# A decoder layer on one core: W_s's row sums, the past rows' sums and the sample's mixing done another way, and the tables of the spatial step loaded later

## The chip, the cores and the metric

The kernel runs on one core of one Trainium2 chip. A core has TensorE (PE in the profile; PEld is its weight load), VectorE (DVE), ScalarE (ACT), GpSimd (POOL) and SyncE (SP), which issues DMAs. Each engine works through its own instructions in order; semaphores make one wait for another. The metric is the device time of one execution in microseconds (us), and the median of several executions is given.

## The reference

One layer works on a prompt of 1024 rows and on 8 sample rows (one new row for each of 8 sequences), 1024 wide, all in float32. Cut to what the change touches:

```python
proj = einsum('bld,de->ble', rmsnorm(h, pre_g), w_in)
u, v, z_a, x_b, z_b, g_a, g_b = split(proj, SPLITS)
vn = layernorm(gelu(v), ln_g, ln_b)
# within chunks of 128 rows, 8 heads of 128 channels
s = einsum('hts,bcshd->bcthd', tril(w_s), vn) + b_s
y_a = gelu(u) * s * silu(z_a)
# trailing windows of 2, 4, 8, 16 rows; a sample's past rows come from state_pool (8, 15, 1024)
pooled = mean_over_window(x_b) - x_b
y_b = (blockdiag(pooled, w_pool) * pool_scale) * silu(z_b)
m = sigmoid(g_a) * (y_a @ w_pa) + sigmoid(g_b) * (y_b @ w_pb)
h = h + rmsnorm(m @ w_out, post_g)
h = h + rmsnorm(sigmoid(rmsnorm(h, ple_in_g) @ w_pg) * (p @ w_ple), ple_out_g)
```

Three small things in it matter here. A sample row is the first row of its chunk, so its mixing is s = w_s[h, 0, 0] * vn + b_s[h, 0]. For the prompt, the scale and the shift of the layer norm are taken out of the mixing: with n the normalised rows, sum over s of W[t, s] * (g * n[s] + b) is g * (W n)[t] + b * rowsum(W)[t], so the row sums of the lower triangle of W_s are wanted once, as an offset `off` = b * rowsum(W_s) + b_s. And a sample's window needs the sum of the last 1, 3, 7 or 15 past rows, by channel group.

## The kernel before

The layer is a stream of about a hundred large products on PE. A product of float32 matrices is computed from two parts of each factor (ACT copies the high part, DVE subtracts it: `split`), three matmuls for each tile. `strassen` (line 632) makes seven products of a projection's pair of 128-column blocks, each accumulated over four k-tiles in one of three PSUM regions (tag `acc`), which DVE (`u<-acc,u`, `v<-acc,u`) or ACT (`u<-acc`) must empty before the region is used again. In its order P1, P6, P2, P7, P4, P5, P3, the last, P3, adds into the region that P5 has just filled and DVE has just read.

The stages follow each other: the four pairs of the v projection (`vsteps`), of the gate g_a (`gasteps`), of u and z_a (`usteps`), of x_b and z_b with the pooling (`bsteps`), of g_b, then the merges and the two last projections. V's output is transposed by the DMA engines: ACT splits it into 16-bit planes `vw`, SP issues one DMA transpose for each of the eight blocks (`v_planes`, 871), ACT joins the planes into `big` (`v_join`, 880) and applies gelu (`v_turn`, 889). In the gate stage the layer norm and the mixing are fitted in (`ln_stats`, `ln_apply`, `spatial`, 984).

Which instruction stands where is decided by a planner (class `Planner`, line 51). Every operation is recorded by `take` (146) with an estimated busy time and, for a DMA, its amount and the time until it has landed; `order` (202) then runs through the estimates and puts each engine's instructions in the order in which they would start. The order is fixed at build time; on the chip only the semaphores decide when something runs. A DMA on SP also waits until the DMA issued eight before it has landed. The first part of the program (`begin`, 1601) is kept in its written order, the rest is free.

The parts that the change touches: `small_tables` (1094, called at 1680 in `begin`) makes on POOL the eight diagonal tables `diag` for the sample's mixing and four 0/1 tables `mask` for the past rows. `ln_loads` (936) loads W_s (`ws`) and the layer norm's vectors, put at the second step of the first v pair (1278). `spatial_weights` (948) clears the upper triangle on POOL, transposes the eight heads on PE into the PSUM banks `psw` and splits them into `wst` (1279). `spatial_offsets` (965) forms the row sums by four products with a tile of ones (`rowsum`) and from them `off`. `sample_spatial` (1001) multiplies the eight sample rows by `diag` (`smix`). `pool_state` (1091) loads the 120 past rows into row block 7 of `big`, and `state_sums` (1112) sums them by eight products with `mask` (`state`) into `past`, which `window` (1132) reads.

Of the kernel before, what the change touches and what calls it, by code (L numbers as in the profile page):

```python
# [15 lines left out]
P = 128  # L16
# [39 lines left out]
class Planner:  # L56
# [89 lines left out]
    def take(self, engine, method, args, kwargs):  # L146
        given = [*(("out" if i == 0 else "", a) for i, a in enumerate(args)), *kwargs.items()]
        writes = [a for k, a in given if k in ("out", "accum_out") and a is not None]
        reads = [a for k, a in given if k not in ("out", "accum_out") and hasattr(a, "tensor")]
        if kwargs.get("accum_op") is not None:  # L150
            reads += writes
        name = writes[0].tensor.name
        if engine == "tensor" and self.open is not None and self.open[0] == name:
            op = self.open[1]
        else:
            op = Op(engine, len(self.ops), self.clock, self.fixed)
            self.ops.append(op)
        self.open = (name, op) if engine == "tensor" else None
        op.calls.append((method, args, kwargs))
        op.spent.append(op.busy)  # L160
        if method[:9] == "dma_start":
            op.busy, op.moved = 1.0 if engine == "gpsimd" else 0.45, writes[0].size() * (2e-6 if writes[0].dtype == U16 else 4e-6)
            op.lands = 4.5 if kwargs.get("accum_op") is not None else 2.0
        else:
            took = self.duration(engine, method, writes[0], reads, kwargs)
            op.busy += took
            if engine == "tensor" and not self.fixed:
                self.clock += took
            if engine == "scalar":
# [134 lines left out]
def hybrid_step(  # L304
# [643 lines left out]
    def spatial_weights():  # L948

        ws = lnt["ws"]  # L950
        nc.gpsimd.affine_select(out=ws, in_=ws, pattern=[[0, NB], [-1, P]], compare_op=ALU.is_ge,
                                fill=0.0, base=0, channel_multiplier=1)
        lnt["wst"] = []
        for h4 in range(0, NB, 4):
            w = slot("wst", (P, 4, 2, P), F32R)
            ps = bank("psw")
            for i in range(4):
                nc.tensor.transpose(ps[:, i * P : (i + 1) * P], ws[:, h4 + i, :], ident)
            split(ps.rearrange("p (h t) -> p h t", t=P), w[:, :, 0], w[:, :, 1])
            lnt["wst"].append(w)  # L960
        ps = bank("lncol")
        nc.tensor.transpose(ps[:, : 2 * NB], lnt["vec"][: 2 * NB, :], ident[: 2 * NB, : 2 * NB])
        nc.vector.tensor_copy(lncol, ps[:, : 2 * NB].rearrange("p (i k) -> p i k", i=2))

    def spatial_offsets():

        ones = slot("ones", (P, P), F32R)
        nc.gpsimd.memset(f32(ones), 1.0)
        off = lnt["off"] = slot("off", (P, NB, P))
        for h4, w in zip(range(0, NB, 4), lnt["wst"]):  # L970
            ps = bank("rowsum")
            for c in range(2):
                nc.tensor.matmul(ps.rearrange("p (h t) -> p h t", t=P), ones, w[:, :, c], start=c == 0, stop=c == 1)
            for h in range(h4, h4 + 4):
                c = slice(h * P, (h + 1) * P)
                nc.vector.scalar_tensor_tensor(out=off[:, h], in0=ps[:, (h - h4) * P : (h - h4 + 1) * P],
                                               scalar=lncol[:, 1, h : h + 1], in1=lnt["bs"][:, c],
                                               op0=ALU.mult, op1=ALU.add)

    def v_split(t):  # L980
        lnv["cut", t] = lnv["cut", t], slot("vl", (P, D), F32R)
# [19 lines left out]
    def sample_spatial():  # L1001
        ps = bank("smix").rearrange("p (h t) -> p h t", h=NB)
        for h in range(NB):
            nc.tensor.matmul(ps[:, h, :NS], sv[:NS, h * P : (h + 1) * P], lnt["diag"][:NS, h, :],
                             start=True, stop=True)
        first = lnt["bs"].rearrange("p (h t) -> p h t", h=NB)[:, :, :1]
        add(smix_s, ps[:, :, :NS], first.to_broadcast([P, NB, NS]))


    kept = {}  # L1010
# [5 lines left out]
    wgcut = {what: dram.tile([HALF, D], F32, tag="wg" + what, name="wg" + what) for what in ('T4', 'B22')}  # L1016
    kept["h"] = dram.tile([T, D], F32, tag="h", name="h")
    kept["e"] = dram.tile([T, D], F32, tag="e", name="e")

# [69 lines left out]
    masks = {}  # L1089

    def pool_state():
        dma(big[: NS * POOL_BUF, 7, :D], state.rearrange("b r d -> (b r) d"))

    def small_tables():

        w00 = lnt["w00"]
        diag = lnt["diag"] = cpool.tile([P, NB, NS], F32, tag="diag", name="diag")
        for h in range(NB):
            nc.gpsimd.tensor_scalar(out=diag[:, h, :], in0=ident[:, :NS], scalar1=w00[:, h : h + 1],
                                    scalar2=None, op0=ALU.mult)  # L1100
        for g, w in enumerate(WINDOWS):
            m = masks[g] = small.tile([P, NS], F32, tag="mask", name=f"mask{g}", bufs=NPAIR)
            nc.gpsimd.memset(m, 1.0)
            nc.gpsimd.affine_select(out=m, in_=m, pattern=[[-POOL_BUF, NS]], compare_op=ALU.is_ge,
                                    fill=0.0, base=w - 1 - POOL_BUF, channel_multiplier=1)
            nc.gpsimd.affine_select(out=m, in_=m, pattern=[[POOL_BUF, NS]], compare_op=ALU.is_ge,
                                    fill=0.0, base=POOL_BUF - 1, channel_multiplier=-1)

    state_sb, tail = big[:, 7, :D], big[:, 6, :D]
    past = cpool.tile([P, NB, NS], F32, tag="past", name="past")  # L1110

    def state_sums():

        n = NS * POOL_BUF
        ps = bank("state").rearrange("p (b t) -> p b t", b=NB)
        for b in range(NB):
            nc.tensor.matmul(ps[:, b, :NS], state_sb[:n, b * P : (b + 1) * P], masks[b // 2][:n, :],
                             start=True, stop=True)
        nc.vector.tensor_copy(past, ps[:, :, :NS])

    class XB(User):
        def tails(self):
# [152 lines left out]
    at(vsteps[1][0], lambda: xop.cut("T4"))  # L1275


    at(c[1], ln_loads)
    at(vsteps[1][2], spatial_weights)
    for i, u in enumerate(vusers):  # L1280

        nxt = vsteps[1][1:] + vsteps[2] if i == 0 else (vsteps[i + 1] if i + 1 < NPAIR else gasteps[0])
# [318 lines left out]
    def begin():  # L1601
# [130 lines left out]
```

## Time and profile before

| | us |
|---|---|
| median of 3 runs | 1000.1 (1000.04 to 1001.04) |
| the profiled execution | 997.51 |
| its span, first to last instruction | 995.8 |
| ACT busy in the span | 526.0 |
| DVE busy in the span | 800.5 |
| idle time of ACT before joining planes, ended by a DMA transpose | 8.4 |

The profile is of one execution, and all its times are from the first instruction of the span. A row of the timeline has start, length, engine, line, operation, tiles written<-read, shapes and a count; in brackets the idle time before it and what ended it. Line 297 is that of the helper that plays the recorded operations, so groups are told apart by their tiles.

### The profile page before, as it was taken

The numbers are of one execution on the slowest core, as the hardware profiler recorded it, in microseconds if no ns is written. First come the engines' busy times: TensorE is split into PE (matmuls) and PEld (weight loads), VectorE is DVE, ScalarE is ACT, GpSimd is POOL, SyncE is SP. The second block draws the span as 40 slices with busy tenths as digits, with TensorE's granted clock in tenths as the row PEclk, the third lists the DMA queues.
The fourth block names the chain that finished last, engine by engine and source line by source line (L and its number), as shares of the span: only waits on it lengthen the run. The fifth ranks groups of instructions, "written<-read, shape, count | busy, mean of one in ns | idle before, by whom it ended". The sixth has DMA issues, their size and how long they took to land. (4 is left out here: it accounts for less than half of the span.)

```text
span 995.8 us, 16069 instructions
## 1 busy us (share of the span) xinstructions
PE 981.3 (99%) x6136; PEld 881.0 (88%) x6136; DVE 800.5 (80%) x1241; ACT 526.0 (53%) x925; POOL 72.7 (7%) x162
## 2 busy tenths in 40 slices
PE   8999999999999999999999999999999999999996
PEld 6889989999999899999999999999999988888885
DVE  5975468777778888888897987697799798779796
ACT  7767888756434434243433343562353365677653
POOL 2200000000000000001000100000000002312111
PEclk9999999999999999999999999999999999999999
DMA  9334462232365355546635166874663553389646
GB/s 342 128 124 85 110 169 106 86 107 64 135 230 186 104 184 185 197 134 227 240 120 166 40 238 232 287 287 149 215 254 110 172 206 68 84 275 364 166 108 191
DMA packets 103970, 171.14 MB, mean 172 GB/s; under 512 B 24254, under 2 KB 64238, under 8 KB 103885
## 3 DMA queue, kind: packets, MB, share of 16 engines
q1 hardware_dynamic: 101525, 162.21, 47.9%
q0 software_dynamic: 2048, 7.37, 4.3%
q8 instruction: 48, 0.79, 0.3%
q10 hardware_dynamic: 320, 0.54, 0.2%
q14 instruction: 29, 0.24, 0.1%
HBM read 114.59 MB, written 51.77 MB: 167 GB/s over the span
## 5 line engine op out<-in xcount | busy, mean ns | idle before, releaser
L297 DVE TENSOR_TENSOR u<-acc,u 128x520 f32<-128x520 f32 (+1 forms) x90 | 62.6, 696 | 38.8 <-PE acc L297 36.8
L297 POOL TENSOR_TENSOR rstd<-ms,mhalf 128x1 f32<-128x1 f32 (+1 forms) x45 | 36.5, 812 | 213.6 <-DVE ms L297 213.5
L297 POOL MEMSET u<- 128x8 f32 x35 | 3.5, 105 | 558.1 <-PE acc L297 310.9
L297 ACT ACTIVATE u<-acc 128x512 f32<-128x512 f32 x39 | 23.2, 595 | 26.9 <-PE acc L297 26.4
L297 ACT ACTIVATE paw<-pas 128x512 fp32r<-128x512 f32 x16 | 10.1, 629 | 31.2 <-DVE pas L297 25.9
L297 ACT ACTIVATE pbw<-pbs 128x512 fp32r<-128x512 f32 x16 | 10.0, 630 | 28.2 <-DVE pbs L297 24.9
L297 DVE TENSOR_TENSOR big<-big 128x1024 f32<-128x1024 f32 (+4 forms) x20 | 23.6, 1217 | 0.0
L297 ACT ACTIVATE big<-v 128x1024 uint16<-128x1024 uint16 x16 | 18.5, 1173 | 8.4 <-DMA v<-vw 8.4
L297 ACT ACT_TABLE_LOAD x15 | 19.2, 1283 | 6.5 <-PE acc L297 5.5
L297 ACT ACTIVATE big<-pht,gvec 128x128 f32<-128x128 f32 x64 | 18.0, 381 | 8.1 <-PE pht L297 8.1
L297 ACT ACTIVATE big<-mix 128x256 f32<-128x256 f32 x32 | 12.2, 384 | 16.9 <-PE mix L297 16.2
L297 PE MATMUL accm<-qh,wpoolw 128*128 128x260 f32 (+1 forms) x96 | 20.9, 320 | 0.0
L297 DVE TENSOR_TENSOR acc<-acc,u 128x512 f32<-128x512 f32 (+1 forms) x16 | 11.2, 699 | 8.8 <-PE acc L297 8.8
L297 DVE TENSOR_TENSOR big<-mix,big 128x256 f32<-128x256 f32 x32 | 13.2, 422 | 5.9 <-ACT big L297 5.0
L297 ACT ACTIVATE zbw<-zbs 128x512 fp32r<-128x512 f32 x16 | 10.1, 632 | 14.6 <-DVE zbs L297 7.2
L297 ACT ACTIVATE zaw<-zas 128x512 fp32r<-128x512 f32 x16 | 10.0, 630 | 14.5 <-DVE zas L297 9.0
L297 ACT ACTIVATE gbw<-gbs 128x512 fp32r<-128x512 f32 x16 | 10.0, 626 | 13.9 <-DVE gbs L297 12.0
L297 PEld LDWEIGHTS accm<-qh,wpoolw 128*128 128x128 f32 x96 | 15.5, 188 | 1.9
L297 ACT ACTIVATE zbw<-zbraw 128x512 fp32r<-128x512 f32 x12 | 7.5, 627 | 17.8 <-DMA zbraw<-in_w_in_dram 16.3
L297 ACT ACTIVATE uw<-us 128x512 fp32r<-128x512 f32 x16 | 10.0, 627 | 12.3 <-DVE us L297 9.8
L297 ACT ACTIVATE junk<-ge 128x512 bf16<-128x512 f32 (+2 forms) x19 | 11.6, 609 | 8.9 <-DVE ge L297 8.3
L297 ACT ACTIVATE gb<-gb 128x1032 f32<-128x1032 f32 (+1 forms) x8 | 6.8, 854 | 17.6 <-DVE gb L297 17.6
(689 smaller groups left out, 3632.2 us busy)
## 6 DMA issues: line engine op xcount, KB each, us to landing
ga<-ga SPq DMA_DIRECT2D x16, 516.0 KB
gb<-gb SPq DMA_DIRECT2D x16, 516.0 KB
ya<-za SPq DMA_DIRECT2D x8, 516.0 KB
yb<-zb SPq DMA_DIRECT2D x8, 516.0 KB
x<-in_x_prompt_dram SPq DMA_DIRECT2D x8, 512.0 KB
vraw<-in_w_in_dram SPq DMA_DIRECT2D x8, 512.0 KB
e<-e SPq DMA_DIRECT2D x8, 512.0 KB
garaw<-in_w_in_dram SPq DMA_DIRECT2D x8, 512.0 KB
```

The source lines that it names most:

```text
L297: getattr(getattr(self.nc, e), method)(*args, **kwargs)
```

## The change

- The planner charges a DMA transpose 3.0 us of its engine (0.45 before), next to no amount, and 1.5 us to land.
- `ln_loads` moves to the fourth step of the third v pair, `spatial_weights` and `ln_rows` to the first step of the gate.
- Row sums of W_s: DVE reduces `ws` along s (128 x 8 sums), SP writes them to DRAM turned (8 x 128) and reads them back to all partitions into `off`; DVE multiplies and adds in place. The tile of ones and the four products go.
- Sample's mixing: eight transposes of the sample rows on PE, then DVE multiplies by w_s[h, 0, 0] and adds b_s[h, 0]. The tables `diag` go.
- Past rows: POOL clears row block 7 of `big`; ten DMAs place the rows that each window needs, for channel block k in partitions 8k to 8k+7 (eight latest rows in partitions 64 and up, earlier ones below); DVE reduces over the eight rows held by a partition; one product with `twice` (two identity blocks side by side, added) sums the two halves and transposes. The tables `mask` go, and `small_tables` with them.

```diff
@@ take
             op.lands = 4.5 if kwargs.get("accum_op") is not None else 2.0
+            if method == "dma_start_transpose":
+                op.busy, op.moved, op.lands = 3.0, 0.01, 1.5
@@ spatial_weights
+        sums = cpool.tile([P, NB], F32, tag="rowsums", name="rowsums")
+        nc.vector.tensor_reduce(out=sums, in_=ws, op=ALU.add, axis=mybir.AxisListType.X)
+        dma(kept["rowsum"].rearrange("h t -> t h"), sums)
@@ spatial_offsets
-        ones = slot("ones", (P, P), F32R)
-        nc.gpsimd.memset(f32(ones), 1.0)
         off = lnt["off"] = slot("off", (P, NB, P))
-        for h4, w in zip(range(0, NB, 4), lnt["wst"]):
-            ps = bank("rowsum")
-            for c in range(2):
-                nc.tensor.matmul(ps.rearrange("p (h t) -> p h t", t=P), ones, w[:, :, c], start=c == 0, stop=c == 1)
...
+        dma(off, kept["rowsum"].partition_broadcast(P))
+        for h in range(NB):
+            nc.vector.scalar_tensor_tensor(out=off[:, h], in0=off[:, h], scalar=lncol[:, 1, h : h + 1],
+                                           in1=lnt["bs"][:, h * P : (h + 1) * P], op0=ALU.mult, op1=ALU.add)
@@ sample_spatial
-            nc.tensor.matmul(ps[:, h, :NS], sv[:NS, h * P : (h + 1) * P], lnt["diag"][:NS, h, :],
-                             start=True, stop=True)
+            nc.tensor.transpose(ps[:, h, :NS], sv[:NS, h * P : (h + 1) * P], ident[:NS, :NS])
         first = lnt["bs"].rearrange("p (h t) -> p h t", h=NB)[:, :, :1]
-        add(smix_s, ps[:, :, :NS], first.to_broadcast([P, NB, NS]))
+        mul(smix_s, ps[:, :, :NS], lnt["w00"].unsqueeze(2).to_broadcast([P, NB, NS]))
+        add(smix_s, smix_s, first.to_broadcast([P, NB, NS]))
@@ pool_state
-        dma(big[: NS * POOL_BUF, 7, :D], state.rearrange("b r d -> (b r) d"))
+        rows_of = big[:, 7, :D].rearrange("p (r c) -> p r c", c=P)
+        nc.gpsimd.memset(rows_of, 0.0)
+        nc.vector.tensor_tensor(out=twice, in0=ident[:, : P // 2], in1=ident[:, P // 2 :], op=ALU.add)
+        for k in range(NB):
+            w = WINDOWS[k // 2] - 1
+            for j in range(2):
+                n = min(w, NB) if j else w - NB
+                if n > 0:
+                    first = POOL_BUF - n if j else POOL_BUF - w
+                    dma(rows_of[(j * NB + k) * NS : (j * NB + k + 1) * NS, NB - n :],
+                        state[:, first : first + n, k * P : (k + 1) * P])
@@ state_sums
-        n = NS * POOL_BUF
-        ps = bank("state").rearrange("p (b t) -> p b t", b=NB)
-        for b in range(NB):
-            nc.tensor.matmul(ps[:, b, :NS], state_sb[:n, b * P : (b + 1) * P], masks[b // 2][:n, :],
-                             start=True, stop=True)
-        nc.vector.tensor_copy(past, ps[:, :, :NS])
+        got = big[:, 4, :P]
+        nc.vector.tensor_reduce(out=got, in_=state_sb.rearrange("p (r c) -> p c r", c=P),
+                                op=ALU.add, axis=mybir.AxisListType.X)
+        ps = bank("state")
+        nc.tensor.matmul(ps[:, : P // 2], got, twice, start=True, stop=True)
+        nc.vector.tensor_copy(past, ps[:, : P // 2].rearrange("p (b t) -> p b t", b=NB))
@@ where the steps are put
-    at(c[1], ln_loads)
-    at(vsteps[1][2], spatial_weights)
+    at(vsteps[2][3], ln_loads)
+    at(gasteps[0][0], spatial_weights)
-    at(vsteps[3][0], ln_rows)
+    at(gasteps[0][0], ln_rows)
@@ begin
-        small_tables()
```

The changed numbers of the planner reorder the instructions from about the second v pair to the end of the gate stage, and a little in the pooling. Two places show it.

SP, from the third transpose of V's planes (`v<-vw`) to the loads of the layer norm's rows; `garaw` are the weights of the first gate pair. Before:

```order
L297 DMA_TRANSPOSE v_287<-vw_307 128x16x128
L297 DMA vraw_310<-in_w_in_dram 128x4x256
L297 DMA_TRANSPOSE v_288<-vw_308 128x16x128
L297 DMA_TRANSPOSE v_314<-vw_329 128x16x128
L297 DMA garaw_334<-in_w_in_dram 128x4x256
L297 DMA garaw_335<-in_w_in_dram 128x4x256
L297 DMA_TRANSPOSE v_315<-vw_330 128x16x128
L297 DMA lng_331<-in_ln_g_dram 128x1024
```

and after the change:

```order
L299 DMA_TRANSPOSE v_282<-vw_297 128x16x128
L299 DMA_TRANSPOSE v_283<-vw_298 128x16x128
L299 DMA ws_308<-in_w_s_dram 128x8x128
L299 DMA lnvec_309<-in_ln_g_dram 8x128
L299 DMA lnvec_309<-in_ln_b_dram 8x128
L299 DMA garaw_323<-in_w_in_dram 128x4x256
L299 DMA garaw_324<-in_w_in_dram 128x4x256
L299 DMA_TRANSPOSE v_304<-vw_321 128x16x128
L299 DMA_TRANSPOSE v_305<-vw_322 128x16x128
L299 DMA lng_351<-in_ln_g_dram 128x1024
```

The two gate loads stood behind the first transpose of the third pair (the fifth of eight) and now stand before it, behind the loads of W_s.

PE at the end of the last v pair: `xT1` is P5, `xB22` is P3, which adds into P5's region, and `gaw` are the gate's weights. Before, P3's last rows and the gate's first product behind them:

```order
L297 MATMUL acc_348<-xT1h_262,vw_338 128x260 x2
L297 MATMUL acc_348<-xB22h_229,vw_341 128x260 x2
L297 MATMUL acc_348<-xB22l_230,vw_341 128x260 x2
L297 MATMUL acc_348<-xB22h_231,vw_341 128x260 x2
L297 MATMUL acc_351<-xB11h_189,gaw_343 128x512
L297 MATMUL acc_351<-xB11l_190,gaw_343 128x512
L297 MATMUL vt_353<-ident,v_339 8x128
```

and after the change (`psw` are the transposes of W_s; rows between these of the same products are left out, here and above):

```order
L299 MATMUL acc_337<-xT1h_257,vw_327 128x260 x2
L299 MATMUL acc_340<-xB11h_191,gaw_332 128x512
L299 MATMUL acc_340<-xB11l_192,gaw_332 128x512
L299 MATMUL acc_337<-xB22h_231,vw_330 128x260 x2
L299 MATMUL acc_337<-xB22l_232,vw_330 128x260 x2
L299 MATMUL psw_344<-ident,ws_308 128x128 x4
L299 MATMUL psw_346<-ident,ws_308 128x128 x4
L299 MATMUL acc_357<-xT2h_241,gaw_334 128x260 x2
```

The gate's first product now stands between P5 and P3, and W_s's transposes, which stood in the second v pair, follow P3.

On DVE the reduction over the past rows stands in front of P5's add of the first x_b pair, whose region is `acc_715`:

```order
L299 TENSOR_TENSOR xb_706<-acc_710,u_697 128x512
L299 TENSOR_REDUCE big<-big 128x128
L299 TENSOR_TENSOR xb_706<-acc_715,u_697 128x520
L299 TENSOR_TENSOR zbw_722<-zbraw_699,zbw_722 128x512
L299 TENSOR_TENSOR zbw_727<-zbs_713,zbw_727 128x512
L299 COPY past<-state_711 128x64
```

Where the reduction stands there was an add of the sums of ya (`za<-za,yalow`) before, and `past` was copied in the same place; that add now comes behind `past`.

More of the change, by code (lines that the diff above doesn't have):

```diff
@@ L965, in spatial_offsets @@
     def spatial_offsets():
-        ones = slot("ones", (P, P), F32R)
-        nc.gpsimd.memset(f32(ones), 1.0)
         off = lnt["off"] = slot("off", (P, NB, P))
-        for h4, w in zip(range(0, NB, 4), lnt["wst"]):
-            ps = bank("rowsum")
-            for c in range(2):
-                nc.tensor.matmul(ps.rearrange("p (h t) -> p h t", t=P), ones, w[:, :, c], start=c == 0, stop=c == 1)
[L974 to L978, printed above, removed]
+        dma(off, kept["rowsum"].partition_broadcast(P))
+        for h in range(NB):
+            nc.vector.scalar_tensor_tensor(out=off[:, h], in0=off[:, h], scalar=lncol[:, 1, h : h + 1],
+                                           in1=lnt["bs"][:, h * P : (h + 1) * P], op0=ALU.mult, op1=ALU.add)
     def v_split(t):
@@ L1016, in hybrid_step @@
     wgcut = {what: dram.tile([HALF, D], F32, tag="wg" + what, name="wg" + what) for what in ('T4', 'B22')}
+    kept["rowsum"] = dram.tile([NB, P], F32, tag="rowsum", name="rowsum")
     kept["h"] = dram.tile([T, D], F32, tag="h", name="h")
@@ L1088, in hybrid_step @@
     q_h, q_l, zbs, yblow = {}, {}, {}, {}
-    masks = {}
+    twice = cpool.tile([P, P // 2], F32, tag="twice", name="twice")
     def pool_state():
-        dma(big[: NS * POOL_BUF, 7, :D], state.rearrange("b r d -> (b r) d"))
[L1094 to L1107, printed above, removed]
+        rows_of = big[:, 7, :D].rearrange("p (r c) -> p r c", c=P)
[9 more added lines that the diff above has]
+                        state[:, first : first + n, k * P : (k + 1) * P])
     state_sb, tail = big[:, 7, :D], big[:, 6, :D]
```

## The prediction

> **What bounds the kernel now.** The page comes first: the share of each engine, and which one has no room.
>
> ```profile
> span 995.8 us, 16069 instructions
> PE 981.3 (99%) x6136; PEld 881.0 (88%) x6136; DVE 800.5 (80%) x1241; ACT 526.0 (53%) x925; POOL 72.7 (7%) x162
> ```
>
> TensorE (PE) is busy 981.3 of 995.8 us. The end of a busy matmul is modelled, so the share alone does not prove that PE sets the time. The view by stretches of 25 us shows where it stands still at all (columns: busy time and instructions of PE, weight load, DVE, ACT, POOL, then granted clock, DMA share, GB/s):
>
> ```profile
> 0.00:25.00 25.00, 20.79 (x116) 17.16 (x117) 14.00 (x28) 19.05 (x31) 7.04 (x29) 1.00 0.99 348
> 25.00:50.00 25.00, 25.00 (x140) 21.29 (x139) 22.56 (x28) 17.36 (x25) 7.07 (x26) 1.00 0.32 124
> ...
> 125.00:150.00 25.00, 23.14 (x155) 20.61 (x154) 16.86 (x30) 22.07 (x39) 0.87 (x3) 1.00 0.67 166
> 150.00:175.00 25.00, 25.00 (x164) 22.86 (x164) 22.62 (x47) 22.20 (x52) 1.61 (x3) 1.00 0.29 106
> ...
> 400.00:425.00 25.00, 25.00 (x172) 23.10 (x171) 20.30 (x34) 5.29 (x9) 0.91 (x4) 1.00 0.54 181
> ```
>
> Outside the start and the last stretch PE loses 1.86 us in 125 to 150 us and almost nothing elsewhere. So there are two ways to a shorter time: work taken from PE's stream, which then closes up, and the waits in 125 to 150. POOL's tables lie in the second stretch, where PE is full all the same: taking them from POOL there is worth nothing. The granted clock is 1.00 throughout; it plays no part.
>
> **The products that go.** PE's timeline, with the row behind each group, gives what the group takes from the stream (start to start; the second column is a modelled length and overlaps the next row):
>
> ```profile
> 148.06 1.95 PE L297 MATMUL smix<-diag,sv 8*128 8x8 f32 x16
> 149.94 0.51 PE L297 MATMUL acc<-xB11h,gaw 128*128 128x512 f32 x1
> ...
> 158.53 1.08 PE L297 MATMUL rowsum<-wst,ones 128*128 128x512 f32 x4
> 159.45 0.39 PE L297 MATMUL acc<-xB21h,gaw 128*128 128x512 f32 x1
> ...
> 404.41 1.85 PE L297 MATMUL state<-mask,big 120*128 120x8 f32 x16
> 406.12 0.48 PE L297 MATMUL acc<-xB11h,zbw 128*128 128x512 f32 x1
> ...
> 17.92 0.38 PE L297 MATMUL pst<-ident,x 128*128 128x128 f32 x2
> 18.23 0.66 PE L297 MATMUL pxe<-ident,xe 8*128 8x8 f32 x8
> 18.82 0.44 PE L297 MATMUL pst<-ident,x 128*128 128x128 f32 x2
> ```
>
> - Row sums of W_s: 159.45 - 158.53 = **0.92 us** go whole.
> - Sample's mixing: 149.94 - 148.06 = 1.88 us for sixteen records (each float32 product is two passes). Eight transposes of the same 8x128 operand shape stand at 18.23: 18.82 - 18.23 = 0.59 us, one record each. Saved: **1.29 us**.
> - Past rows: 406.12 - 404.41 = 1.71 us, 0.107 us a pass. The one product left has two passes over 64 columns instead of 8, which no row shows. Below it costs two of these passes, 0.21; above, two passes of a 128-column float32 instruction, 0.31 by the pair of transposes at 17.92 (the next row starts at 18.23). I take 0.23, near the first, since it streams 64 columns. Saved: **1.48 us** (1.40 to 1.50).
>
> Sum 0.92 + 1.29 + 1.48 = 3.69 us of PE's stream. The eight transposes of W_s only move; they cost PE the same in the new place.
>
> **The wait in 125 to 150.** The timeline of PE, DVE and SP:
>
> ```profile
> 126.86 0.39 PE L297 MATMUL acc<-xB22h,vw 128*128 128x260 f32 x1 [1.40 <-DVE v L297]
> ...
> 134.16 0.51 PE L297 MATMUL acc<-xT2h,gaw 128*128 128x260 f32 x2 [0.32 <-DVE gaw L297]
> ...
> 119.86 0.70 DVE L297 TENSOR_TENSOR u<-acc,u 128x520 f32<-128x520 f32 x1 [5.18 <-PE acc L297]
> 125.51 0.69 DVE L297 TENSOR_TENSOR gas<-garaw,garaw 128x512 f32<-128x512 f32 x1 [4.95 <-DMA garaw<-in_w_in_dram]
> 126.12 0.69 DVE L297 TENSOR_TENSOR v<-acc,u 128x520 f32<-128x520 f32 x1
> ...
> 104.22 14.24 SPq L297 DMA_TRANSPOSE v<-vw  x2
> 118.55 1.76 SPq L297 DMA_DIRECT2D garaw<-in_w_in_dram  x2
> ```
>
> The chain reads backwards: the product with xB22 adds into the region that `v<-acc,u` must empty; that add stands on DVE behind `gas<-garaw,garaw`, which waits for weights that SP issued only at 118.55, because a transpose that was not ready stood ahead of them from 104.22. The change cuts this twice, as the two places of the order show: the garaw loads now stand ahead of that transpose (the planner charges it 3 us of SP instead of 0.45), and PE has the first gate product between the two, some 2.8 us of cover by the rows (twelve 512-column products at 0.23, as the rowsum row has four in 0.92). I take the 1.40 as gone. The rest of the 1.86 I leave standing, since W_s's steps now come just here.
>
> What comes in: ACT two copies and DVE two subtractions, a copy and the reduction.
>
> ```profile
> L297 ACT ACTIVATE wst<-psw x2: 572/586/600, 76.4 to 79.4; 128x512 fp32r<-128x512 f32 x2
> L297 DVE TENSOR_TENSOR wst<-psw,wst x2: 683/688/692, 77.0 to 80.8; 128x512 fp32r<-128x512 f32 x2
> L297 DVE COPY lncol<-lncol x1: 167/167/167, 82.0 to 82.0; 128x16 f32<-128x16 f32 x1
> ...
> 157.62 0.15 DVE L297 TENSOR_REDUCE vsum<-vsums 128x1 f32<-128x4 f32 x1
> ...
> 157.94 1.22 DVE L297 TENSOR_TENSOR lastv<-lastv,lnb 128x1024 f32<-128x1024 f32 x1
> ```
>
> That is 1.17 us on ACT (22.07 of 25 busy there) and 1.38 + 0.17 on DVE, plus a reduction over 1024 elements that the trace does not show: one over 4 elements takes 0.15, an add over 1024 takes 1.22, so 0.15 to 2.4 (twice the add); I take 1.2, the add's. DVE has 8.1 us free in this stretch, so it hides 2.8; ACT has 2.9 free and hides 1.2, with little to spare. POOL's select and the three loads before it only move: the loads leave SP ahead of the gate weights, and those are wanted two products of 2.8 us before W_s's transposes, so the select (1.5 us) is done in time. The sums' store adds one issue to SP (0.36 by the rows below) ahead of the last two transposes; they were not what PE waited for. The second instruction of the sample's mixing and the add for `twice` (0.2 us each, little over the smallest rows) lie in DVE's free time.
>
> **The state step's new chain.** Before, one load was issued 10 us ahead of its products. Now memset, ten loads, a reduction and one product follow each other after the last reader of that row of `big`:
>
> ```profile
> 393.12 1.22 DVE L297 TENSOR_TENSOR za<-za,big 128x1024 f32<-128x1024 f32 x1
> 402.34 0.68 DVE L297 TENSOR_TENSOR zbs<-zbraw,zbs 128x512 f32<-128x512 f32 x1
> ...
> 394.37 0.36 SPq L297 DMA_DIRECT2D big<-in_state_pool_dram  x1
> ...
> L297 POOL MEMSET u<- 128x8 f32 x35 | 3.5, 105 | 558.1 <-PE acc L297 310.9
> ...
> L297 POOL MEMSET ones<- x1: 208/208/208, 139.7 to 139.7; 128x128 f32 x1
> L297 SPq DMA_DIRECT2D ws<-in_w_s_dram x1: 389/389/389, 57.6 to 57.6; - x1
> L297 POOL TENSOR_SCALAR_AFFINE_SELECT ws<-ws x1: 1524/1524/1524, 63.0 to 63.0; 128x1024 f32<-128x1024 f32 x1
> ```
>
> `big` is free at 394.34. The memset over 1024 elements takes at most eight times the 0.208 of one over 128, 1.7, and 0.9 to 1.0 if the fixed part is the 0.105 of those over 8; I take 1.0: 395.4. Ten issues at 0.36 and a gap of 0.05: 399.5. The last load lands between 2 and 5.4 us later (5.4 is ws, 512 KB, from issue to its user at 63.0; these are small): 401.5 to 404.9. DVE reaches the reduction behind the 402.34 row, at 403.0, and needs 1.2: 404.2 to 406.1. PE wants the product at 404.41. So it waits 0 to 1.7 us, to 3.0 with the reduction at its upper bound. I take 0, near the small loads' end. Behind the reduction on DVE stands the add that empties the next region (due 404.61); behind the loads on SP stand only stores of `ya` and its sums, for which nothing waits here. The reduction reads with a step of 512 bytes. The Trainium skill, "SBUF — State Buffer", section "Door 1: The DMA port swizzle", says that an access pattern which goes to a new 16-byte line with every element pays a penalty; it gives no price, no row here shows one, and by it the case of the long wait below would be the likelier.
>
> **Sum.** 3.69 + 1.40 = 5.09 us off the profiled execution, whose own time is 997.51 (span 995.8 and 1.7 around it): 992.4. The runs shown have a median of 1000.1, 2.6 above it, so the same gain there gives **995.0**.
>
> **The rivals.**
> - *The boundary wait stays or comes back* (chance 0.16): ACT, 22 of 25 us busy, is late with the gate weights or with W_s's copies, and PE waits again. Then only the products count: 1000.1 - 3.69 = 996.4. For it, ACT's load there and 1.2 more; against it, the earlier weights.
> - *The state chain is late* (0.13): 1.0 to 3.0 us of new wait, 996.0 to 998.0, and with the boundary wait too, up to 999.4.
> - *DVE stands at the offsets* (0.08), the one that ends slower. `off` now comes through DRAM: 1024 pieces of 4 bytes are written, and the read-back leaves SP behind the store of lastv.
>
> ```profile
> 159.18 0.36 SPq L297 DMA_DIRECT2D out_dram<-lastv  x1
> 162.67 2.16 DVE L297 SCALAR_TENSOR_TENSOR off<-rowsum,lncol,bsb 128x128 f32<-128x128 f32 x8
> ```
>
>  Issued at 159.6 and 5.4 us under way, it lands at 165. DVE works in order and comes to its first offset some 7 us after lastv, at about 166. Each us beyond that stops DVE, and PE after one more product (2.8). To be slower by 2 us than before, the read must land 5.1 + 2.0 + 2.8 = 9.9 us after DVE wants it, at 176: three times the 5.4. The result would be 1002.1 or more. The Trainium skill, "DMA: Bandwidth & Descriptors", section "Specifications", says that transfers under 512 B are read, modified and written; the write here has 20 us before the read, so by it the case is possible and no more.
> - *PE's records mislead* (0.09): PE would have waited for DVE or DMA soon after each removed group, and the time is 999 to 1000.1. Against it: 25.00 of 25 busy in the stretches around 158 and 404.
>
> **How the numbers follow.** The forecast (0.54) is 995.0, from 993.5 (the whole 1.86 gone, and a little of the other waits) to 996.2. To hold eight in ten, the range takes in the second case and most of the third with a measurement's 0.3: 993.3 to 999.0. A measurement of this kernel tells 0.2%, 2 us, from no change. Below 998.1 lie the forecast, the first rival and two thirds of the second: 0.79. Within lie 0.13, and slower 0.08.
>
> **What would show it.** In the changed profile: smix takes 0.6 us on PE, state 0.2 to 0.3, rowsum has no row on PE; PE in 125 to 150 is busy 24.5 or more, and garaw leaves SP ahead of the fifth of the eight transposes, near 110. A wait of PE for DVE at the state product shows the second rival; idle time of DVE for a DMA of `off` near 165 the third. The prediction is wrong if PE shows new idle time of over 3 us in any stretch.

## The result, and the profile after

| | before | after |
|---|---|---|
| median of 6 runs, us | 1000.07 (998.30 to 1001.04) | **994.67** (993.25 to 996.09) |
| ratio, 95% interval | | 0.9944 (0.9927 to 0.9962) |
| the profiled execution, us | 997.51 | 993.25 |
| its span, us | 995.8 | 991.5 |

The prediction was 995.0, in 993.3 to 999.0, faster: right. By the profiled executions the gain is 4.26 us against 5.09 predicted; by the medians it is 5.4, with 3.8 to 7.3 by the interval.

The page after, and the view by stretches (columns as before):

```profile
span 991.5 us, 16004 instructions
...
PE 977.7 (99%) x6110; PEld 878.0 (89%) x6110; DVE 802.9 (81%) x1245; ACT 522.8 (53%) x923; POOL 69.6 (7%) x142
```

```profile
125.00:150.00 25.00, 24.72 (x164) 21.95 (x163) 15.78 (x31) 21.30 (x41) 0.65 (x2) 1.00 0.71 150
300.00:325.00 25.00, 24.20 (x157) 21.85 (x157) 23.56 (x36) 10.87 (x18) 0.21 (x2) 1.00 0.38 132
400.00:425.00 25.00, 24.74 (x162) 22.44 (x162) 22.96 (x38) 7.09 (x11) 0.10 (x1) 1.00 0.52 181
```

PE has 26 instructions fewer. In 125 to 150 it loses 0.28 us where it lost 1.86; in 400 to 425, full before, it now loses 0.26, and in 300 to 325 0.80 (0.52 before). PE's timeline at the two places where products went:

```profile
145.77 0.66 PE L299 MATMUL smix<-ident,sv 8*128 8x8 f32 x8
146.71 0.50 PE L299 MATMUL acc<-xB11h,gaw 128*128 128x512 f32 x1 [0.28 <-ACT gaw L299]
...
400.66 0.40 PE L299 MATMUL acc<-xT1h,xbw 128*128 128x260 f32 x2
401.32 0.43 PE L299 MATMUL state<-twice,big 128*128 128x64 f32 x2 [0.26 <-DVE big L299]
401.56 0.48 PE L299 MATMUL acc<-xB11h,zbw 128*128 128x512 f32 x1
```

The sample's mixing takes about 0.6 of PE, then PE waits for gate weights from ACT (start to start 0.94; the 0.28 in brackets counts from a modelled end). The state's product takes 0.24 start to start, and PE stands before it: the two rows ahead should be 0.24 apart, as two products of that width are elsewhere, and are 0.66 apart, so the wait is 0.42. What it waits for is on DVE, where the reduction stands between two adds that empty PE's regions:

```profile
398.68 0.69 DVE L299 TENSOR_TENSOR xb<-acc,u 128x512 f32<-128x512 f32 x1
399.28 1.98 DVE L299 TENSOR_REDUCE big<-big 128x128 f32<-128x1024 f32 x1
401.18 0.69 DVE L299 TENSOR_TENSOR xb<-acc,u 128x520 f32<-128x520 f32 x1
```

It starts on time, right behind the add ahead of it, so its loads were not late; it is long. SP's timeline, and the groups of `rowsums` and `off`:

```profile
107.47 0.94 SPq L299 DMA_DIRECT2D garaw<-in_w_in_dram  x2
113.56 4.50 SPq L299 DMA_TRANSPOSE v<-vw  x2
...
128.39 0.38 SPq L299 DMA_DIRECT2D rowsum<-rowsums  x1
133.79 6.44 SPq L299 DMA_TRANSPOSE v<-vw  x2
...
160.57 1.61 SPq L299 DMA_DIRECT2D off<-rowsum  x1
```

```profile
L299 DVE TENSOR_REDUCE rowsums<-ws x1: 1211/1211/1211, 127.2 to 127.2; 128x8 f32<-128x1024 f32 x1
L299 DVE SCALAR_TENSOR_TENSOR off<-off,lncol,bsb x8: 341/344/350, 168.2 to 176.9; 128x128 f32<-128x128 f32 x8
```

The first gate weights leave SP at 107.47 where they left at 118.55. The sums' store of 128.39 stands just ahead of the last two transposes. DVE never waits for `off`.

To compare kernels, the table takes from each timeline the start of the first product with the weights `vw`, `uw`, `xbw` and `zbw`: the first two bound the stage of v and the gate, the last two the state's stage. "Waits" sums PE's waits over 0.15 us in the first stage, each as start to start of two products less the usual distance. "Low clock" is the time lost to stretches of lower granted clock in that stage (below). Each ratio is to the kernel before in the same round of runs. Its medians were 1000.07 (after), 998.51 (the three parts, charge and moves), 998.63 (old charge, tables early, 512-byte store, three adds) and 999.21 (charge alone, moves alone, both), so across rounds the ratios are compared, not the medians. Beside the three later medians 994.67 would be a gain of 3.8 to 4.5 us, nearer the profiles' 4.26 than the 5.4 of its own round.

| kernel | v and gate, us | its waits | low clock | state, us | median | ratio (95%) |
|---|---|---|---|---|---|---|
| before | 193.35 | 2.36 | 0 | 21.51 | | 1 |
| after | 188.99 | 0.57 | 0 | 20.53 | 994.67 | 0.9944 (0.9927 to 0.9962) |
| only sample's mixing | 197.48 | 6.13 | 1.7 | 21.5 | 1003.63 | 1.0052 (1.0032 to 1.0072) |
| only past rows | 193.20 | as before | 0 | 20.44 | 998.60 | 1.0003 (0.9988 to 1.0019) |
| only row sums | 199.86 | 7.66 | 1.7 | 21.5 | 1004.32 | 1.0057 (1.0038 to 1.0077) |
| charge and moves | 190.72 | 0 | 0 | 21.57 | 996.65 | 0.9978 (0.9965 to 0.9992) |
| charge alone | 190.77 | 0 | 0 | 21.58 | 996.14 | 0.9969 (0.9954 to 0.9983) |
| moves alone | 190.74 | 0 | 0 | 21.57 | 998.00 | 0.9985 (0.9975 to 0.9996) |
| after, old charge | 195.25 | 4.26 | 2.5 | 20.50 | 999.42 | 1.0003 (0.9991 to 1.0016) |
| after, tables early | 195.99 | 5.3 | 1.7 | 20.46 | 999.86 | 1.0011 (0.9997 to 1.0024) |
| after, 512-byte store | 190.79 | 1.96 | 0 | 20.44 | 995.17 | 0.9961 (0.9946 to 0.9976) |
| after, three adds | 188.75 | 0.35 | 0 | 20.02 | 993.67 | 0.9942 (0.9924 to 0.9961) |
| after, both | 190.81 | 1.95 | 0 | 19.98 | 994.37 | 0.9955 (0.9940 to 0.9971) |

Each line closes: waits, plus low clock, less the products removed, less the 2.36 of before, gives the stage's change within 0.5 us. For the changed kernel it is 0.57 - 2.36 - 0.92 - 1.29 = -4.00; measured -4.36.

### The profile page after: what moved, and what is told of

It reads as the page before. It is cut to its first block, busy times and chain, and to the rows that moved or that the text cites. A ratio compares the mean times of both kernels' runs of the same rounds, so it can differ in the third digit from the quotient of the medians.

```text
span 991.5 us, 16004 instructions
## 1 busy us (share of the span) xinstructions
PE 977.7 (99%) x6110; PEld 878.0 (89%) x6110; DVE 802.9 (81%) x1245; ACT 522.8 (53%) x923; POOL 69.6 (7%) x142
## 5 line engine op out<-in xcount | busy, mean ns | idle before, releaser
L299 DVE TENSOR_TENSOR v<-acc,u 128x520 f32<-128x520 f32 (+1 forms) x9 | 6.3, 697 | 13.4 <-PE acc L299 13.4
L299 ACT ACTIVATE vw<-v 128x1024 uint16<-128x1024 uint16 x16 | 16.1, 1045 | 0.5 <-DVE v L299 0.5
```

What stands on the lines that cost most here:

```text
L299: getattr(getattr(self.nc, e), method)(*args, **kwargs)
```

## The experiments

**One part of the change at a time, in the kernel before.**

```diff
-            nc.tensor.matmul(ps[:, h, :NS], sv[:NS, h * P : (h + 1) * P], lnt["diag"][:NS, h, :],
-                             start=True, stop=True)
+            nc.tensor.transpose(ps[:, h, :NS], sv[:NS, h * P : (h + 1) * P], ident[:NS, :NS])
...
+        mul(smix_s, ps[:, :, :NS], lnt["w00"].unsqueeze(2).to_broadcast([P, NB, NS]))
+        add(smix_s, smix_s, first.to_broadcast([P, NB, NS]))
```

> The kernel before with only the sample's mixing done by eight transposes, and the tables diag gone. Theory (PE's stream closes up over what is taken from it): smix takes 0.6 us of PE instead of 1.88, the span is 1.3 us shorter, ratio 0.9987, the wait of 1.4 us near 126 us stays. Rival (PE would have waited soon after anyway; the gain of the whole change comes from the new order alone): smix is shorter on PE, but PE's idle time grows by the same amount and the span stays within 0.3 us.

Measured: slower by 5.1 us (1003.63 against 998.51). The eight transposes are as short as expected; the planner's new order is what costs. PE's timeline, and the row of DVE's that ends its wait:

```profile
127.92 0.51 PE L297 MATMUL acc<-xB22h,vw 128*128 128x260 f32 x2 [1.89 <-DVE v L297]
128.26 0.58 PE L297 MATMUL acc<-xB22l,vw 128*128 128x260 f32 x2
128.65 1.07 PE L297 MATMUL acc<-xB22h,vw 128*128 128x260 f32 x4
...
156.08 1.08 PE L297 MATMUL rowsum<-wst,ones 128*128 128x512 f32 x4
...
159.89 0.36 PE L297 MATMUL mix<-wst,vh 128*128 128x256 f32 x1 [2.73 <-DVE off L297]
```

```profile
158.62 2.15 DVE L297 SCALAR_TENSOR_TENSOR off<-rowsum,lncol,bsb 128x128 f32<-128x128 f32 x8
```

The first mixing now stands right behind the row-sum products, and PE waits 2.73 until DVE has made `off` out of their banks (before, 5.7 us of other products lay between, 159.45 to 165.11). The boundary wait of 126 us grew to 1.89, and behind it four products of 260 columns take 0.86 instead of 0.48, which is the low clock (last column but two of the view by stretches):

```profile
128.00:132.00 4.00, 4.00 (x21) 4.00 (x22) 2.40 (x5) 3.67 (x7) 0.00 (x0) 0.57 1.00 325
```

So a removed 1.29 us brought 3.8 us of waits and 1.7 of clock. Neither the theory nor the rival had this.

```diff
-            nc.tensor.matmul(ps[:, b, :NS], state_sb[:n, b * P : (b + 1) * P], masks[b // 2][:n, :],
-                             start=True, stop=True)
+        nc.vector.tensor_reduce(out=got, in_=state_sb.rearrange("p (r c) -> p c r", c=P),
+                                op=ALU.add, axis=mybir.AxisListType.X)
...
+        nc.tensor.matmul(ps[:, : P // 2], got, twice, start=True, stop=True)
```

> The kernel before with only the past rows' sums done by ten loads, a reduction and one product, and the tables mask gone. Theory: state takes 0.2 to 0.3 us of PE instead of 1.71, less a wait of PE of 0.4 us for the reduction as in the changed kernel: 1.0 us shorter, ratio 0.9990. Rival: span unchanged, PE idle 1.4 us more around 404.

Measured: the state's stage is 1.07 us shorter and nothing else moves; 1.07 is 1.48 less a wait of about 0.4 for the reduction, as in the changed kernel. The time shows no difference (1.0003), which at an interval of 1.5 us either way can't exclude it.

```diff
+        nc.vector.tensor_reduce(out=sums, in_=ws, op=ALU.add, axis=mybir.AxisListType.X)
+        dma(kept["rowsum"].rearrange("h t -> t h"), sums)
...
-                nc.tensor.matmul(ps.rearrange("p (h t) -> p h t", t=P), ones, w[:, :, c], start=c == 0, stop=c == 1)
```

> The kernel before with only W_s's row sums moved from PE to DVE and DRAM, tables loaded early as before. Theory: 0.9 us shorter, ratio 0.9991, no row of rowsum on PE. Rival: unchanged, or longer if DVE stands at the offsets for the read from DRAM (idle time of DVE for a DMA of off).

Measured: slower by 5.8 us. The tables still come early, so the 4-byte store stands right ahead of the first transposes. SP's timeline, and the view of ACT's waits from 60 to 160 us (total, times, longest), here and before:

```profile
81.09 0.38 SPq L297 DMA_DIRECT2D rowsum<-rowsums  x1
81.56 19.09 SPq L297 DMA_TRANSPOSE v<-vw  x2
```

```profile
ACT big L297 <- DMA v<-vw: 14.0, 4, 9.9
```

```profile
ACT big L297 <- DMA v<-vw: 8.4, 4, 4.2
```

By the semaphores in the trace the store's last piece lands 9.9 us after its issue, and the transpose behind it 10.4 us after its own, where a transpose with nothing ahead of it needs 4 to 5. ACT waits 9.9 us for those planes, and PE five times for what ACT and DVE then deliver late (0.9 to 2.1 us each, 93 to 135 us).

**The order alone.**

```diff
+            if method == "dma_start_transpose":
+                op.busy, op.moved, op.lands = 3.0, 0.01, 1.5
-    at(c[1], ln_loads)
-    at(vsteps[1][2], spatial_weights)
+    at(vsteps[2][3], ln_loads)
+    at(gasteps[0][0], spatial_weights)
-    at(vsteps[3][0], ln_rows)
+    at(gasteps[0][0], ln_rows)
```

> The kernel before with only the planner's new charge for DMA transposes and the tables' steps moved; all products as before. Theory: PE's instructions are the same in number, the wait of 1.40 us near 126 goes, the stretch 125 to 150 has PE busy 24.5 or more instead of 23.1: 1.4 us shorter, ratio 0.9986. Rival (the order is the whole gain): 4 to 5 us shorter, ratio 0.995 to 0.996.

Measured: 996.65 against 998.51. All products are as before, and all of PE's waits from 75 to 175 us are gone, not only the one at 126: the view by stretches has PE full.

```profile
100.00:125.00 25.00, 25.00 (x166) 22.87 (x165) 14.38 (x21) 22.52 (x47) 1.72 (x2) 1.00 0.51 125
125.00:150.00 25.00, 25.00 (x171) 22.93 (x171) 15.04 (x28) 21.41 (x41) 0.82 (x3) 1.00 0.50 131
```

The stage is 2.63 us shorter: more than the theory's 1.4, less than the rival's 4 to 5.

**Charge or moves.** The kernel before with the two added lines alone,

```diff
+            if method == "dma_start_transpose":
+                op.busy, op.moved, op.lands = 3.0, 0.01, 1.5
```

> The kernel before with one line of the change: the planner reckons 3 us of SP for a DMA transpose. All products and tables as before. In the written order the first gate weights now leave SP ahead of the fifth transpose, as they also do with only the moved tables' steps. Theory (either of the two edits is enough for the wait at 126 us, because both bring these weights forward): the 1.40 us wait there is gone, the other waits of 93 to 150 us (1.2 us together in the kernel before, the transposes' planes behind the tables) stay in part; 997.5 to 998.8 where the kernel before takes 1000, and the stage from the first spatial product to u's first product lasts 191.5 to 192.5 us where the kernel before takes 193.35 and the kernel with both edits 190.7. Rival (the charge does all of the order's gain, 2.6 us): that stage lasts 190.7 and the time is as with both edits, 996.7. Rival (the charge does nothing in this order): 1000 and 193.3.

and with the three moved lines alone:

```diff
-    at(c[1], ln_loads)
-    at(vsteps[1][2], spatial_weights)
-    at(vsteps[3][0], ln_rows)
+    at(vsteps[2][3], ln_loads)
+    at(gasteps[0][0], spatial_weights)
+    at(gasteps[0][0], ln_rows)
```

> The kernel before with the tables' steps moved to later due times, and nothing else: charge and products as before. In the written order four transposes now leave SP ahead of W_s's load, and the first gate weights ahead of the fifth. Theory (the moves do most of the order's gain): the stage from the first spatial product to u's first product lasts 190.7 to 191.5 us (193.35 before), the wait at 126 us and the waits for the transposed planes near 93 to 150 us are gone, 996.7 to 997.5 where the kernel before takes 1000. Rival (the charge does it): this kernel keeps 1 us or more of waits in 93 to 150 us and takes 998.5 or more.

Measured: 190.77 and 190.74 for the stage, the same as both together, and no wait left in it. By the profiles either is enough, and the gains don't add up. For the charge the rival was right and the theory too small. For the moves the theory was right in the stage; the time, 998.0, lies between its 997.5 and the rival's 998.5. In both, SP's timelines have the gate weights ahead of the fifth transpose.

```profile
113.64 0.97 SPq L299 DMA_DIRECT2D garaw<-in_w_in_dram  x2
117.52 1.98 SPq L299 DMA_TRANSPOSE v<-vw  x1
```

```profile
106.83 1.03 SPq L297 DMA_DIRECT2D garaw<-in_w_in_dram  x2
112.95 4.57 SPq L297 DMA_TRANSPOSE v<-vw  x2
```

The times differ by more than the profiles (996.14 and 998.00). The mean granted clock of the moves' other ten runs was 0.993 to 0.995, and that of the profiled one 0.997; where the clock fell in those ten, no profile shows.

In all kernels here that lost the wait near 126 us, PE also has the gate's first product between P5 and P3; in the four that kept it (before and the three single parts) neither holds. Which of the two would be enough, no run separates.

**The changed kernel without the charge.**

```diff
-            if method == "dma_start_transpose":
-                op.busy, op.moved, op.lands = 3.0, 0.01, 1.5
```

> The changed kernel with the planner's old charge for DMA transposes. Theory (the moved tables, not the charge, bring the gate weights forward and put the gate's first product between P5 and P3): the wait near 126 stays away, PE busy 24.5 or more in 125 to 150, time within 0.1% of the changed kernel, ratio to the kernel before 0.994 to 0.996. Rival (the charge does it): the wait of 1.4 us is back, ratio 0.996 to 0.9975.

Measured: 999.42, the whole gain gone, which neither the theory nor the rival had. The gate weights are still ahead of the fifth transpose and there is no wait at 126 us, as the theory said; a later one took its place. PE's timeline, and the view by stretches:

```profile
146.36 0.40 PE L297 MATMUL acc<-xB11l,gaw 128*128 128x512 f32 x1
150.85 1.22 PE L297 MATMUL acc<-xB11h,gaw 128*128 128x512 f32 x2 [4.09 <-DVE gaw L297]
```

```profile
151.00:156.00 5.00, 5.00 (x14) 4.04 (x15) 3.60 (x11) 4.29 (x8) 0.55 (x1) 0.50 0.00 0
```

DVE's and SP's timelines show what it waits for:

```profile
148.18 0.69 DVE L297 TENSOR_TENSOR gas<-garaw,garaw 128x512 f32<-128x512 f32 x1 [6.49 <-DMA garaw<-in_w_in_dram]
```

```profile
136.34 0.50 SPq L297 DMA_DIRECT2D garaw<-in_w_in_dram  x1
136.90 5.51 SPq L297 DMA_TRANSPOSE v<-vw  x1
142.51 0.51 SPq L297 DMA_DIRECT2D garaw<-in_w_in_dram  x1
```

It is the wait of before, one pair later: the second half of the next gate weights stands on SP behind the last transpose, whose issue alone takes 5.51 us, and DVE stands 6.49 us at them with `ga<-acc,u` and `gaw` queued behind. PE waits 4.26 us and then works for 5 us at half the clock. In the changed kernel both halves leave together at 140.34, behind both transposes, and there DVE waited 1.87. Behind the store of 4-byte pieces (127.42 here) the last two transposes land 7.0 and 9.8 us after their issue (7.2 and 8.3 in the changed kernel).

That the last transpose parts the two halves does not make the wait by itself. With the moves alone, also without the charge, SP has the same order:

```profile
135.32 0.50 SPq L297 DMA_DIRECT2D garaw<-in_w_in_dram  x1
136.37 3.16 SPq L297 DMA_TRANSPOSE v<-vw  x1
139.65 0.51 SPq L297 DMA_DIRECT2D garaw<-in_w_in_dram  x1
```

There the transpose holds SP for 3.16 us, the second half has landed at 144.58 instead of 148.16, and PE does not wait. Two things differ: no store of 4-byte pieces stands ahead of it, and ahead of the waited-for product PE has 2.4 us of row-sum and sample products, here 0.6. Which counts for more was not separated.

**The changed kernel with the tables early.**

```diff
-    at(vsteps[2][3], ln_loads)
-    at(gasteps[0][0], spatial_weights)
-    at(gasteps[0][0], ln_rows)
+    at(c[1], ln_loads)
+    at(vsteps[1][2], spatial_weights)
+    at(vsteps[3][0], ln_rows)
```

> The changed kernel with the tables loaded and W_s prepared early, where they were before. Theory (the row sums' store of 1024 pieces of 4 bytes holds the DMA transposes that follow it by some 5 us, as it did when this edit was made alone): ACT waits 9 to 10 us for the first transposes of V's planes near 82, PE idles in the stretch 75 to 125 by 3 to 6 us, ratio 0.998 to 1.004. Rival (the wait there came from the old charge): ACT waits under 5 us there, ratio 0.994 to 0.996.

Measured: 999.86. Again the store stands ahead of the first transposes (81.05 on SP), ACT waits 10.3 us for the planes, and PE 1.67, 1.51 and, at 153.29, 1.96 us, the last with the low clock behind it. The theory held. So moving the tables later is not only a gain by itself; the row sums by DRAM need it.

**The store in rows of 512 bytes.**

```diff
-        dma(kept["rowsum"].rearrange("h t -> t h"), sums)
+        nc.tensor.transpose(ps[:NB, :P], sums, ident)
+        nc.vector.tensor_copy(turned[:NB], ps[:NB, :P])
+        dma(kept["rowsum"], turned[:NB])
```

> The changed kernel with the row sums turned by one transpose on PE and stored as eight rows of 512 bytes. Theory (the 4-byte store delays the last two transposes by 2 to 3 us, and with them ACT): the store lands in 2 to 3 us, the seventh transpose is back in under 5 us from its issue, the wait of PE for ACT at the sample's mixing (0.4 us) goes, PE has 0.2 us more work: 0.2 to 0.5 us shorter than the changed kernel, ratio to before 0.9940. Rival: the late transposes are hidden, and the kernel is 0.1 to 0.3 us longer for the added transpose.

Measured: the store lands within 1.2 us of its issue (11.0 in the changed kernel), the transpose behind it 5.0 after its own (7.2), ACT's waits for planes fall from 4.7 to 2.4. And the time is no better (0.9961): in the new order PE waits 0.95 at 146.47 for DVE's `ga` and 0.50 at 159.81 for `vl`. What the late transposes cost PE in the changed kernel this run does not tell, since the order changed with the store; by the table it is not more than the 0.57 of waits there.

**Three adds instead of the reduction.**

```diff
-        nc.vector.tensor_reduce(out=got, in_=state_sb.rearrange("p (r c) -> p c r", c=P),
-                                op=ALU.add, axis=mybir.AxisListType.X)
+        rows = state_sb.rearrange("p (r c) -> p r c", c=P)
+        add(rows[:, :4], rows[:, :4], rows[:, 4:])
+        add(rows[:, :2], rows[:, :2], rows[:, 2:4])
+        add(got, rows[:, 0], rows[:, 1])
```

> The changed kernel with the past rows reduced by three adds of neighbouring halves (512, 256, 128 elements), which read without a large step. Theory (the reduction's 1.98 us against 1.21 for the same count read in a row is the price of the 512-byte step): the three adds take 1.3 us together, PE's wait at the state product (0.4 to 0.7 us) shrinks to under 0.1, 0.4 to 0.6 us shorter than the changed kernel. Rival (the reduction is long for another reason, or something else ends that wait): the wait stays.

Measured: timelines of DVE and PE,

```profile
398.90 1.47 DVE L299 TENSOR_TENSOR big<-big 128x512 f32<-128x512 f32 x3
...
400.28 0.40 PE L299 MATMUL acc<-xT1h,xbw 128*128 128x260 f32 x2
400.52 0.34 PE L299 MATMUL state<-twice,big 128*128 128x64 f32 x2
400.67 0.47 PE L299 MATMUL acc<-xB11h,zbw 128*128 128x512 f32 x1
```

1.47 us instead of 1.98 (1.3 expected), and the wait before the product is gone: the state's stage is 20.02, now 1.49 below before. 993.67 is the lowest median of all; from the changed kernel (0.9942 beside 0.9944) the times can't tell it, the stage in the trace can.

**Both.**

```diff
+        nc.tensor.transpose(ps[:NB, :P], sums, ident)
+        nc.vector.tensor_copy(turned[:NB], ps[:NB, :P])
+        dma(kept["rowsum"], turned[:NB])
...
+        add(rows[:, :4], rows[:, :4], rows[:, 4:])
```

> The changed kernel with both side prices taken out: the row sums are turned by one product on TensorE and stored as 8 rows of 512 bytes, and the past rows are reduced by three adds of unbroken rows. Theory (the two edits act in different stages and add up): the state's stage lasts 20.0 us as with the adds alone (20.5 in the changed kernel), and the stage of v and the gate lasts 190.8 us as with the rows alone (189.0 in the changed kernel), since the waits that the planner's new order adds stay: 994.7 to 995, no better than the changed kernel, and 1 us behind the adds alone. Rival (the waits that the 512-byte store left were chance of one run): 992.9 to 993.3, better than the adds alone.

Measured: 190.81 and 19.98 us for the stages: the effects of the two edits add up, the waits that the 512-byte store's order brings come back at the same places, and the rival falls. 994.37, no better than the adds alone.

## Why the prediction was right, and where it was off

- **PE is the bound; what leaves its stream closes up.** Right. The row sums and the sample's mixing were to give 0.92 + 1.29 = 2.21. The changed kernel's stage is 1.73 shorter than that of the order alone (190.72 - 188.99), and 0.57 of waits stand in it: 2.3. But this held only together with the order. Alone, each of the two edits made the kernel 5 to 6 us slower.
- **The state step.** 1.48 predicted, 0.98 got. The product is right (0.24 beside 0.23); the step that failed is "a reduction of 1.2, the add's" and so "I take 0" for the wait. The loads were in time, as taken; the reduction took 1.98 and made PE wait 0.42. The second rival's mechanism was there, at less than its 1 us. The row: 1024 elements in memory order take 1.21 (`rowsums`), with a step of 512 bytes 1.98, 0.77 more. The Trainium skill, "SBUF — State Buffer", section "Door 1: The DMA port swizzle", says that a new 16-byte line with every element costs a penalty; the trace agrees in direction. That the step is the cause is not shown: the two reductions also differ in their number of results, 8 in each partition there and 128 here.
- **The boundary wait.** 1.40 predicted as gone, "the rest of the 1.86 I leave standing". This term was mis-sized: the rest went as well, 2.6 us in the order alone, 1.2 more than taken. Its explanation was half right. The wait went with the gate weights ahead of the fifth transpose and the gate's first product between P5 and P3, as it said; but it put the first down to the planner's charge, and the moves alone do it too. The row that it reads as one transpose from 104.22 on holds two, the fourth at 104.22 and the fifth at 116.72; the fifth is the one that was not ready.
- **What the charge is for** in the changed kernel the prediction did not see: without it the second pair's weights are parted by the last transpose, which holds SP for 5.51 us, and PE waits 4.26 us at 150.85.
- **"They were not what PE waited for"**, of the two transposes behind the sums' store. Nearly right in the changed kernel: the store delays them by about 2 us, and of PE's waits only the 0.57 in the gate stage can come of it, since the gate weights that PE waits for at 146.71 left SP behind them. It is the order that keeps it small: with the early tables ACT waits 10.3 us for the first planes behind the store.
- **New waits taken as 0.** Together 0.57 in the gate stage, where the first rival's mechanism (gate weights late from ACT) was there with 0.41 us, and 0.42 at the state, and the one at 321 us (before 0.69 us, there before too) is 0.96.
- **DVE at the offsets** did not happen. The read was issued at 160.57, needs about 6 us by the trace's semaphores, and its first user starts at 168.2.

The sum came out near because errors cancel, which is luck: 5.09 predicted, 1.2 more from the order, 1.3 less by the new waits (0.57 + 0.42 + 0.3), and 0.7 less by the start and the end of the program, which were that much longer in the changed kernel's profiled execution: 4.3, measured 4.26.

Left open: the tail, from PE's last product to the end of the span, is 7.7 to 9.3 us in these profiles, and no edit explains it. A version with another order behind the 512-byte store was not tried.

## What to carry to other kernels

Where a planner decides the order, a change has two prices: the work it removes, read from the timeline, and the order that comes out, which only the next trace shows; here two edits that lost 5 to 6 us each when made alone gained 1.7 together with the new order. Test an order change by itself, with all the work left in: here it was half of what the two stages gained (2.63 of 5.34 us). A store in small pieces is cheap where it is waited for late, and dear for the DMA that is issued behind it.

## What the runs showed of the hardware

**Some waits of PE cost more than their length, and not by their length alone.** Where the granted clock falls in the middle of a trace, it is 0.50 for 3.4 us (128.3 to 131.7 with only the sample's mixing, 154.1 to 157.5 with the tables early) or for 6.8 (149.4 to 156.2 with the old charge, of which PE works 5), so 3.4 x 0.5 = 1.7 us more are lost each time, or 2.5. Ahead of these falls PE had waited 2.05, 1.96 and, still waiting, 2.6 us. But waits of 2.73 us (only the sample's mixing, ended at 159.89) and 2.14 us (only row sums, ended at 134.60) were followed by a clock of 1.00, as was the 1.56 of the kernel before, 1.40 in its brackets.

What tells them apart may be where they lie. The changes of the clock in a trace are multiples of 3.41 us apart (with only row sums 10.82, 14.24, 157.6 and 161.0). Continued in these steps, the 2.14 us are cut at 133.70 into 1.08 and 0.90 of idle time, and the 2.73 at 159.03 into 1.87 and 1.25 with the next wait; the falls came after steps with 1.89, 1.82 and 2.61 idle. So idle time alone does not set it: 1.87 in a step was followed by no fall and 1.82 was, and with only the row sums the clock fell at 157.6 after a step with no idle time at all, but with the sixteen small products of the sample's mixing; eight of these stand in the 1.82 step too. That the amount of PE's work in a step counts would fit; no run tests it.

The Trainium skill, "TensorE: Matmul & The Clock Gate", section "Part 1: The HAM clock gate (the "warmup" mystery)", says that the clock is halved after an idle window of about 3.4 us, and that the window runs free of the program. Half the clock and the steps of 3.4 us agree; here a window idle for about half of it was enough.

**The start goes with the clock too.** The stretch from 10 to 15 us, in the changed kernel and in the one with the charge alone, whose first spatial product starts at 26.67 and 27.96:

```profile
10.00:15.00 5.00, 4.78 (x20) 3.60 (x21) 3.63 (x8) 4.63 (x10) 2.37 (x3) 1.00 1.03 400
```

```profile
10.00:15.00 5.00, 4.24 (x12) 3.28 (x12) 4.35 (x8) 5.00 (x10) 2.00 (x3) 0.66 1.02 399
```

Of thirteen profiles five have 0.66 there and a start of 27.8 to 28.2 us; the others have 1.00 and 26.1 to 26.7. The same shows in the times: the changed kernel's six runs are 993.25 to 993.79 at a mean granted clock of 0.997 to 0.998, and 995.55 to 996.09 at 0.995 to 0.996. Where the clock fell in the runs without a profile is not shown, but a difference of 2 us between two single executions of this kernel may be this alone, so stages were compared, not spans.

**1024 pieces of 4 bytes.** The store lands in 9.9 to 12.2 us, the same 4 KB as 8 rows of 512 bytes in 1.2 to 1.6. The Trainium skill, "DMA: Bandwidth & Descriptors", section "Specifications", names transfers under 512 bytes as read, modified and written; the runs agree in direction and show what it says nothing of here, that a DMA transpose issued behind the store lands some 2 us later (7.2 against 5.0) to 5 us later (10.4 against 5.3 for the first one before).
